# Hybrid encoder trunk: queries and keys stacked in DRAM and fetched by one ScalarE transfer per operand, and the second norm's sum moved into the second FFN pair

## The chip, the cores and the metric

The kernel runs on one core of one Trainium2 chip. The core has five engines that run side by side: TensorE (PE: matmuls; PEld: the loads of its stationary operand), VectorE (DVE), ScalarE (ACT), GpSimd (POOL) and SyncE (SP), which here only issues transfers. Transfers between DRAM and on-chip memory (SBUF) run on 16 DMA engines; SyncE, ScalarE and GpSimd can each issue them, each through a queue of its own. TensorE writes its sums to eight PSUM banks.

The metric is the device time of one execution in microseconds, the median of several runs. Lower is better.

## The reference

Two layers over a sequence of 512 positions with 1024 channels, in float32. Each layer normalises, projects, feeds three branches, merges them with gates, and ends in a gated FFN:

```python
h = rmsnorm(x, norm1_g[l])
u = h @ w_in[l]                       # q, k, v, GLU input, Fourier input
q = apply_partial_rope(rmsnorm(q, qnorm_g[l]), cos, sin)
k = apply_partial_rope(rmsnorm(k, knorm_g[l]), cos, sin)
att = diff_attention(q, k, v, lam)    # softmax of component 0 minus lam * softmax of component 1
att = rmsnorm(att, subln_g[l]) * (1.0 - lam_init)
y_a = att.reshape(b, s, WIDTH_A) @ w_proj_a[l]
...                                   # y_b: GLU, depthwise convolution, LayerNorm, swish; y_c: 2-D Fourier mixing
merged = gates[:, :, 0] * y_a + gates[:, :, 1] * y_b + gates[:, :, 2] * y_c
x = x + merged @ w_out[l]

h2 = rmsnorm(x, norm2_g[l])
f_gate, f_up = jnp.split(h2 @ w_ffn_in[l], 2, axis=-1)
x = x + (jax.nn.silu(f_gate) * f_up) @ w_ffn_out[l]
```

There are 8 heads, each with two components of 32 dimensions and 64 value dimensions. The FFN is 2816 wide.

## The kernel before

**Precision.** TensorE multiplies fast in a rounded float32 format. Each operand is therefore split into a high part and the rest (`split`, L156: a copy on ScalarE, L159, and a subtraction on VectorE, L160), and each product is three matmuls: high by high, high by low, low by high.

**Weights.** They come in chunks of 128 x 1024 (512 KB) on SyncE's queue (`chunk`, L203, tile wr), are cast to the high part on ScalarE (wh, L208), and the low part is made on VectorE (wl, L210) or, for every second chunk of the middle stages, by a cast on ScalarE (L330) and an adding transfer of GpSimd (L331). There are two buffers for the raw chunk, three for the high and four for the low part.

**Order.** The program is written as one main stream of matmuls with a running time `self.t`. Each instruction gets the due time that holds when it is written (`at`); side work such as the attention is put into a list of events with due times (`later`, `poll`) and is written between the main stream's matmuls when its time has come. A planner then puts the instructions of each engine in an order by due time and by when it holds their inputs to be ready. The order is fixed when the kernel is built; each engine runs its own in order, and the waits between engines are semaphores. Transfers belong to the order of the engine that issues them.

**Queries and keys.** `qkv` (L747) computes q, k and v with the positions on the partitions. `qk_post` (L782) normalises and rotates q and k, and `turn` (L831) transposes each group of 128 channels (two heads) and splits it into tiles at, high and low. Both parts are stored in two DRAM tensors of 128 x 512 on SyncE's queue (dqk<-at, L842). Before each head, `stack` (L850) loads for each of its two components the stacked operands: qst holds the 32 rows of the high, the low and again the high part, kst those of the high, again the high and the low part. A single matmul over 96 rows then gives the three products' sum. Each operand is three loads of 32 rows (64 KB) on SyncE's queue (L859), so there are twelve loads for each head. qst and kst have three buffers each. A load of the second component waits until the head before has finished its scores of the first component.

**Scores.** `scores` (L933) runs, for each of four query blocks, the two score matmuls into PSUM banks s (two of them), takes the maximum on VectorE (L942) and the exponential on ScalarE (L944, tile at). The attention of a layer is spread as events over the Fourier branch, the gates and the convolution branch. `drain` (L571) writes what is left of it ahead of the attention's output projection.

**Attention projection.** `gemm_two` (L237) computes the first two of eight output tiles together: the steps over the first three head pairs for both banks, then the last head pair's step for both. The banks are main, of which there are three. The other six tiles follow one by one (L580). `merge` (L680) gates each (L688) and adds it on GpSimd (L689).

**FFN.** The first FFN matrix is multiplied by a scheme of seven products instead of eight on halves of the matrices. `pair_weights` (L290) makes the seven weight operands of one of 22 pairs; `pair_gemm` (L370) runs four products, copies one bank (p15, L389 and L390) and runs the last three, on two PSUM banks that take turns: tag s for pairs 0, 3, 6 and so on, tag att for 1, 4, ..., main for 2, 5, .... So pair 3 needs the banks of pair 0. `unit` (L605) evacuates a pair: VectorE reads the banks (L608 to L614) and multiplies by rb2, the second norm's factor for each position.

**Second norm.** The square sums of x are added up on GpSimd (L416, tile acc). `inv_rms` (L419) adds them over the partitions by a matmul with ones into bank oth and computes the factor by one operation on VectorE (L426), two on ScalarE (L428, L430) and two on VectorE (L431, L432). It is written after all of pair 1 (L634), and pairs 0 and 1 are evacuated after it.

Of the kernel before, what the change touches and what calls it, by code (L numbers as in the profile page):

```python
# [9 lines left out]
F32 = mybir.dt.float32  # L10
# [6 lines left out]
P = 128  # L17
L = 2
D = 1024
T = 512  # L20
NT = T // P
KT = D // P
# [13 lines left out]
QS = ("sync",) * 4  # L36
# [21 lines left out]
LAG_N = 5000  # L58
LAG_S = 20000
LAST = (2500, 8000)  # L60
LN = (6000, 14000, 29000)
PEORD = False
CONV_LOW = -20000
# [30 lines left out]
class Hybrid:  # L94
# [139 lines left out]
        self.at(self.t)  # L234
        return ps

    def gemm_two(self, xs):  # L237
        banks = [self.bank(), self.bank()]
        n = len(xs)
        ws = [[self.wtile() for _ in xs] for _ in banks]  # L240
        for ks in (range(n - 1), (n - 1,)):
            for ps, w in zip(banks, ws):
                for k in ks:
                    wh, wl = w[k]
                    xh, xl = xs[k]
                    self.at(self.t)
                    self.mm(ps, wh, xh, k == 0, False)
                    self.mm(ps, wh, xl, False, False)
                    self.lastmm = self.mm(ps, wl, xh, False, k == n - 1)
                    self.t += 3 * PASS  # L250
                    self.poll()
        self.at(self.t)
        return banks
# [113 lines left out]
                out[n] = (hi[:, s], lo[:, s])  # L367
        return out

    def pair_gemm(self, u, w, xc, split_k=False):  # L370
        nc = self.nc
        tag = ("s", "att", "main")[u % 3]
        b1, b2 = self.bank(tag), self.bank(tag)
        h = T // 2
        n = len(xc)

        def x(name):
            return [p[name] for p in xc]

        first = (  # L380
            (b1[:, 0:h], "a11", "b11", True), (b1[:, h:T], "s1", "t1", False),
            (b2[:, h:T], "s3", "t3", True), (b2[:, 0:h], "s2", "t2", False),
        )
        steps = (list(range(n - 1)), [n - 1]) if split_k else (list(range(n)),)
        for ks in steps:
            for i, (ps, a, b, start) in enumerate(first):
                self.product(ps, w[a], x(b), ks, start and ks[0] == 0, i % 2 == 1 and ks[-1] == n - 1)
        p15 = self.slot("M")
        nc.scalar.copy(p15, b1)  # L389
        nc.vector.tensor_tensor(out=p15, in0=b2, in1=p15, op=ALU.add)  # L390
        ks = list(range(n))
        self.product(b1[:, 0:h], w["a12"], x("b21"), ks, False, False)
        self.product(b1[:, h:T], w["s4"], x("b22"), ks, False, True)
        self.product(b2[:, h:T], w["a22"], x("t4"), ks, False, True)
        return b1, b2, p15
# [153 lines left out]
    def main(self, l):  # L549
        nc = self.nc  # L550
# [15 lines left out]
        for m in range(KT):  # L566
            py = self.gemm(self.cvs)
# [6 lines left out]
        def merge_a(m, py):  # L574
            self.merge(m, ths[m], py)
            ms.append(self.split_to(merged[m], "cv" if m < 4 else "A"))

        for m, py in enumerate(self.gemm_two(self.atts)):
            merge_a(m, py)
        for m in range(2, KT):  # L580
            merge_a(m, self.gemm(self.atts))
        self.by_dma = False
        x2, xc, acc = [None] * KT, [], None
        g2 = self.par(l, "g2")
        h = T // 2
        for q in range(KT // 2):
            us = self.wtp.tile([P, 2, T], F32, tag="wth", name=self.nm("us"))
            ts = self.wtp.tile([P, 2, T], F32, tag="wtl", name=self.nm("ts"))
            for i, m in enumerate((q, q + KT // 2)):
# [4 lines left out]
                ps = self.gemm(ms)  # L594
# [3 lines left out]
                acc = self.sq_add(xt, acc, "M")  # L598
# [2 lines left out]
        self.xg, self.acc = [], None  # L601
        xin = []
        rb2 = None

        def unit(j, b1, b2, qw, scaled):  # L605
            z = self.slot("M")
            v = nc.vector.tensor_tensor
            v(out=z[:, 0:h], in0=b1[:, 0:h], in1=rb2[:, 0:h], op=ALU.mult)  # L608
            v(out=z[:, h:T], in0=b1[:, h:T], in1=qw[:, 0:h], op=ALU.add)
            v(out=z[:, h:T], in0=z[:, h:T], in1=rb2[:, h:T], op=ALU.mult)  # L610
            nc.scalar.activation(z, z, AF.Silu)
            u = self.slot("M")
            v(out=u[:, 0:h], in0=b2[:, h:T], in1=qw[:, 0:h], op=ALU.add)
            v(out=u[:, h:T], in0=qw[:, 0:h], in1=qw[:, h:T], op=ALU.add)  # L614
            if scaled:
                v(out=u, in0=u, in1=rb2, op=ALU.mult)
            v(out=u, in0=u, in1=z, op=ALU.mult)
            if j < 4:
                t = self.wtp.tile([P, 2, T], F32R, tag="wth" if j < 2 else "wtl", name=self.nm("act"))
                return self.split(u, t[:, 0, :], t[:, 1, :])  # L620
            return self.split_to(u, "att")

        done = 0
        for rnd, nj in enumerate(ROUNDS):
            act = []
            held = []
            scaled = done + nj == NJ
            for j in range(nj):
                w = self.pair_weights(done + j)
                held.append((j, *self.pair_gemm(done + j, w, xc, done + j == 0), scaled))  # L630
                if done + j == 0:
                    continue
                if done + j == 1:
                    rb2 = self.inv_rms(acc, D, "ar", "rb", True)  # L634
                while held:
                    act.append(unit(*held.pop(0)))
            done += nj
            for m in range(KT):
                if scaled and l == L - 1 and m == KT - 1:
                    self.last_tile(m, act, x2[m])  # L640
                    continue
                y = ps = self.gemm(act)
                if not scaled:
                    y = self.slot("M")
                    nc.vector.tensor_tensor(out=y, in0=ps, in1=rb2, op=ALU.mult)  # L645
                nc.vector.tensor_tensor(out=x2[m], in0=y, in1=x2[m], op=ALU.add)
                if done < NJ:
                    continue
                if l == L - 1:
                    nc.sync.dma_start(self.out[m], x2[m])  # L650
                else:
                    sc = self.dram.tile([P, T], F32, tag=f"x{l}_{m}", name=f"x{l}_{m}")
                    getattr(nc, QS[3]).dma_start(sc, x2[m])
                    xin.append(sc)
                    self.next_x(l + 1, m, x2[m])
# [126 lines left out]
    def qk_post(self, l, which, banks):  # L782
        nc = self.nc
# [3 lines left out]
        for i in range(2):  # L787
            tab = self.small(NT * 8, f"tab{i}")
            nc.vector.tensor_tensor(
                out=tab.rearrange("p (t d) -> p t d", d=8), in0=self.rope[:, i],  # L790
# [3 lines left out]
        for tt in range(NT):  # L794
# [6 lines left out]
            f = self.small(16, f"qf{tt}", 1)  # L801
            fa = self.small(16, f"qa{tt}", 1)
            nc.vector.tensor_reduce(
                out=sums, in_=sq.rearrange("p (m d) -> p m d", d=DC), axis=AX.X, op=ALU.add
# [3 lines left out]
                out=sums, in0=sums, scalar1=1.0 / DC, scalar2=EPS, op0=ALU.mult, op1=ALU.add  # L808
# [5 lines left out]
                out=q3, in0=q3, in1=f.unsqueeze(2).to_broadcast([P, 16, DC]), op=ALU.mult  # L814
# [10 lines left out]
        gc = self.small(1, f"gc{which}")  # L825
# [3 lines left out]
        out = []  # L829

        def turn(gp):  # L831
            ps = self.bank("att")
            for tt in range(NT):
                self.pin(
                    nc.tensor.transpose(  # L835
                        ps[:, tt * P : (tt + 1) * P], qs[tt][:, gp * P : (gp + 1) * P], self.ident
                    )
                )
            pair = []
            for i, src in enumerate(self.split_to(ps, "at", scale=gc)):  # L840
                d = self.dram.tile([P, T], F32, tag=f"qk{which}{gp}{i}", name=self.nm("dqk"))
                getattr(nc, QS[1]).dma_start(d, src.bitcast(F32))  # L842
                pair.append(d)
            out.append(pair)

        for gp in range(4):
            self.later(self.t + QKT + gp * 2000, "qk", lambda gp=gp: turn(gp))
# [2 lines left out]
    def stack(self, h):  # L850
        hp, h2 = divmod(h, 2)
        out = []
        for c in range(2):
            row = []
            for which, order in ((0, (0, 1, 0)), (1, (0, 0, 1))):
                dst = self.slot("kst" if which else "qst", F32R)
                lo = h2 * 64 + c * 32
                for r, hl in enumerate(order):
                    getattr(self.nc, QS[0]).dma_start(  # L859
                        dst[r * 32 : (r + 1) * 32, :].bitcast(F32), self.scr[which][hp][hl][lo : lo + 32, :]  # L860
                    )
                row.append(dst)
            out.append(row)
        return out

    def heads(self, l, t0, span):
# [45 lines left out]
        def norm(hp):  # L912
            fs[hp] = self.head_cols(atts[hp], zs.pop(hp))
            self.t += 860
# [5 lines left out]
        for u in range(NH * NT):  # L920
# [7 lines left out]
            if u % 8 == 7:  # L928
                dn, ds = (LAG_N, LAG_S) if u < NH * NT - 1 else LAST
                self.later(t + LAG_T + LAG_V + dn, "att", lambda hp=u // 8: norm(hp))  # L930
# [166 lines left out]
    def conv(self, l, t0, span):  # L1097
# [82 lines left out]
        def up(fn):  # L1180
            self.at(self.tc.cur_priority - LN_UP)
            fn()

        t1 = t0 + span + PAUSE[1]
        for fn, dt in zip((ln0, ln1, ln2), LN):
            self.later(t1 + dt, "conv", lambda fn=fn: up(fn))
# [136 lines left out]
```

## Time and profile before

| | us |
|---|---|
| median of 3 runs | 1625.27 |
| lowest and highest run | 1622.42, 1626.29 |
| the profiled execution | 1623.3 |
| its span, first to last instruction | 1621.5 |
| TensorE busy | 1593.5 |
| VectorE busy | 1309.1 |
| ScalarE busy | 870.6 |
| GpSimd busy | 183.6 |

The mean granted TensorE clock of the profiled execution is 0.993 of full speed.

The profile is of one execution. A line like L126 is the line of the kernel that issued an instruction; where a helper issues it, all its uses have that line, and the tiles (out<-in) tell them apart. PE, DVE, ACT and POOL are the engines' names in it, and a q behind a name (SPq) is the queue on which that engine issues transfers. Busy matmuls overlap, so TensorE's busy time says only that work was in it.

### The profile page before, as it was taken

What the parts mean: (1) busy time and instruction counts of PE and PEld (TensorE: products, weight loads), DVE (VectorE), ACT (ScalarE), POOL (GpSimd) and SP (SyncE); (2) the same over time, 40 slices, a digit from 0 to 9 for tenths busy, and PEclk for the clock granted to TensorE, in tenths of its full rate; (3) what the DMA queues carried; (4) which work ended last, traced back from release to release, by engine and by line L of the source; (5) the groups of instructions that cost most, each with busy time, mean ns of one, the idle gap of its engine ahead of it and who ended that gap; (6) DMA issues with size and microseconds to landing.
All of it is one profiled execution on the core that took longest, in us unless ns stands there. A gap on an engine that the chain in (4) does not pass through costs nothing.

```text
span 1621.5 us, 24447 instructions
## 1 busy us (share of the span) xinstructions
PE 1593.5 (98%) x9104; PEld 1395.3 (86%) x9104; DVE 1309.1 (81%) x2388; ACT 870.6 (54%) x1419; POOL 183.6 (11%) x162
## 2 busy tenths in 40 slices
PE   9999999999998999999999999999999899999999
PEld 7888888787888898999888888887878898989998
DVE  6999999775887786858779999996758878878684
ACT  6546556873565463535444565577635644546351
POOL 1000010113230000000100000020232300000000
PEclk9999999999999999999999999999999999999999
DMA  6556366455463554647432664554445535546361
GB/s 220 169 165 197 83 163 150 112 127 124 150 168 79 156 131 124 150 111 186 127 117 80 196 180 118 137 147 111 119 116 162 144 92 151 136 130 157 87 161 65
DMA packets 80471, 222.85 MB, mean 137 GB/s; under 512 B 11216, under 2 KB 12368, under 8 KB 80352
## 3 DMA queue, kind: packets, MB, share of 16 engines
q1 hardware_dynamic: 67392, 175.59, 34.5%
q0 software_dynamic: 12528, 45.17, 16.2%
q8 instruction: 72, 1.18, 0.3%
q10 hardware_dynamic: 432, 0.53, 0.1%
q14 instruction: 47, 0.39, 0.1%
HBM read 207.35 MB, written 13.89 MB: 136 GB/s over the span
## 4 chain that ended last, share of the span: by engine, by line
PE 92%; DVE 3%; DMA 2%; ACT 1%; issue 1%; SPq 0%; DVEq 0%; ACTq 0%
PE main L126 54%; PE s L342 10%; PE att L342 8%; PE main L342 8%; PE s L126 4%; PE att L126 3%; PE oth L126 3%; PE att L136 2%; DMA cv<-in_w 1%; DMA wr<-in_w 0%; PE att L835 0%; DVE wl L210 0%; DVE A L160 0%; DMA V<-in_xT 0%; DMA kst<-dqk 0%
## 5 line engine op out<-in xcount | busy, mean ns | idle before, releaser
L208 ACT CAST wh<-wr 128x1024 fp32r<-128x1024 f32 x178 | 186.2, 1050 | 244.2 <-PE main L126 130.5
L126 PE MATMUL main<-X,wh 128*128 128x512 f32 x864 | 278.6, 395 | 0.0
L210 DVE TENSOR_TENSOR wl<-wr,wh 128x1024 fp32r<-128x1024 f32 x138 | 176.6, 1280 | 37.6 <-ACT wh L208 37.0
L126 PEld LDWEIGHTS main<-X,wh 128*128 128x128 f32 x864 | 161.0, 189 | 32.5 <-issue 0.3
L1120 DVE SCALAR_TENSOR_TENSOR cv<-cv,hcw,cv 128x497 f32<-128x497 f32 (+14 forms) x240 | 180.4, 752 | 0.9
L126 PE MATMUL main<-X,wl 128*128 128x512 f32 x432 | 169.9, 393 | 0.0
L126 PE MATMUL main<-act,wh 128*128 128x512 f32 (+1 forms) x520 | 161.9, 391 | 0.0
L944 ACT ACTIVATE at<-s,mx 128x512 f32<-128x512 f32 x128 | 87.9, 688 | 59.0 <-DVE mx L942 50.2
L126 PEld LDWEIGHTS main<-act,wh 128*128 128x128 f32 x520 | 96.3, 188 | 21.7 <-DVE M L645 0.6
L126 PE MATMUL main<-A,wh 128*128 128x512 f32 x320 | 107.7, 393 | 0.0
L309 POOL DMA_DIRECT2D wlo<-in_w x44 | 37.8, 859 | 577.7 <-ACT wlo L308 172.9
L126 PE MATMUL main<-att,wh 128*128 128x512 f32 x320 | 100.0, 393 | 3.0 <-ACT att L159 3.0
L942 DVE TENSOR_REDUCE mx<-s 128x1 f32<-128x512 f32 x128 | 86.6, 683 | 19.3 <-PE s L126 18.7
L126 PE MATMUL main<-act,wl 128*128 128x512 f32 (+1 forms) x260 | 101.4, 391 | 0.0
L126 PE MATMUL main<-wh,X 128*128 128x512 f32 x288 | 96.7, 392 | 0.0
L126 PEld LDWEIGHTS main<-X,wl 128*128 128x128 f32 x432 | 81.5, 189 | 16.5
L331 POOL DMA_DIRECT2D wl<-in_w x40 | 34.5, 864 | 518.9 <-ACT wl L330 357.2
L126 PE MATMUL main<-cv,wh 128*128 128x512 f32 x240 | 76.8, 392 | 0.0
L126 PEld LDWEIGHTS main<-att,wh 128*128 128x128 f32 x320 | 59.7, 188 | 17.4 <-ACT att L159 3.5
L126 PE MATMUL main<-A,wl 128*128 128x512 f32 x192 | 74.4, 390 | 0.0
L126 PEld LDWEIGHTS main<-A,wh 128*128 128x128 f32 x320 | 59.7, 188 | 11.9
L126 PEld LDWEIGHTS main<-wh,X 128*128 128x128 f32 x288 | 53.8, 188 | 11.1
(371 smaller groups left out, 4206.7 us busy)
## 6 DMA issues: line engine op xcount, KB each, us to landing
wr<-in_w SPq DMA_DIRECT2D x222, 512.0 KB, 3.8
wlo<-in_w POOLq DMA_DIRECT2D x44, 512.0 KB, 5.6
wl<-in_w POOLq DMA_DIRECT2D x40, 512.0 KB, 7.6
cv<-in_w SPq DMA_DIRECT2D x80, 256.0 KB, 4.7
dqk<-at SPq DMA_DIRECT2D x32, 256.0 KB, 4.6
qst<-dqk SPq DMA_DIRECT2D x96, 64.0 KB, 2.2
kst<-dqk SPq DMA_DIRECT2D x96, 64.0 KB, 2.0
V<-in_xT SPq DMA_DIRECT2D x8, 256.0 KB, 7.1
```

Source lines behind the costliest of these rows:

```text
L126: return self.pin(self.nc.tensor.matmul(out, lhsT=lhsT, rhs=rhs, start=start, stop=stop))
L136: self.pin(self.nc.tensor.transpose(ps[:, s], src[:, s], self.ident))
L208: nc.scalar.copy(hi, raw)
L210: nc.vector.tensor_tensor(out=lo, in0=raw, in1=hi.bitcast(F32), op=ALU.subtract)
L309: nc.gpsimd.dma_start(l2, src2, accum_op=ALU.add)
L331: self.nc.gpsimd.dma_start(lo, src, accum_op=ALU.add)
L342: self.nc.tensor.matmul(ps, lhsT=a[:, s], rhs=b, start=start and k == ks[0] and i == 0, stop=last and i == 2, skip_group_check=True,)
L942: nc.vector.tensor_reduce(out=mx, in_=ps, axis=AX.X, op=ALU.max, negate=True)
L944: nc.scalar.activation(e, ps, AF.Exp, bias=mx, accum_out=z1 if c else z0)
L1120: ins = nc.vector.scalar_tensor_tensor(out=acc[:, a:b], in0=g[:, a + d : b + d], scalar=w[:, t : t + 1], in1=acc[:, a:b], op0=ALU.mult, op ...
```

## The change

Four edits.

- `gemm_two` becomes `gemm_few` with a number of banks, and is called with three: the first three output tiles of the attention projection share the steps over the first three head pairs, and the loop over the others begins at the fourth.
- `pair_gemm` takes a function `mid` that it calls after its first four products. For pair 1 this is `norm`, which writes the second norm's sum and factor with a due time 15000 before the running one (EARLY, in the same unit as `self.t`, in which a full matmul counts 216). The evacuations of pairs 0 and 1 stay where they were.
- `turn` stores one DRAM tensor of 3 x 128 x 512 for each group of 128 channels: three stores of 256 KB on SyncE's queue, of high, low, high for the queries and high, high, low for the keys.
- `stack` loads each operand by one transfer of 3 x 32 rows (192 KB) into the 96 partitions, issued by ScalarE.

```diff
+EARLY = 15000
...
-    def gemm_two(self, xs):
-        banks = [self.bank(), self.bank()]
+    def gemm_few(self, xs, few):
+        banks = [self.bank() for _ in range(few)]
...
-    def pair_gemm(self, u, w, xc, split_k=False):
+    def pair_gemm(self, u, w, xc, split_k=False, mid=None):
...
+        if mid is not None:
+            mid()
         p15 = self.slot("M")
...
-        for m, py in enumerate(self.gemm_two(self.atts)):
+        for m, py in enumerate(self.gemm_few(self.atts, 3)):
             merge_a(m, py)
-        for m in range(2, KT):
+        for m in range(3, KT):
             merge_a(m, self.gemm(self.atts))
...
+        def norm():
+            nonlocal rb2
+            self.at(self.t - EARLY)
+            rb2 = self.inv_rms(acc, D, "ar", "rb", True)
+            self.at(self.t)
...
-                held.append((j, *self.pair_gemm(done + j, w, xc, done + j == 0), scaled))
+                held.append((j, *self.pair_gemm(done + j, w, xc, done + j == 0, norm if done + j == 1 else None), scaled))
                 if done + j == 0:
                     continue
-                if done + j == 1:
-                    rb2 = self.inv_rms(acc, D, "ar", "rb", True)
...
-            pair = []
-            for i, src in enumerate(self.split_to(ps, "at", scale=gc)):
-                d = self.dram.tile([P, T], F32, tag=f"qk{which}{gp}{i}", name=self.nm("dqk"))
-                getattr(nc, QS[1]).dma_start(d, src.bitcast(F32))
-                pair.append(d)
-            out.append(pair)
+            pair = self.split_to(ps, "at", scale=gc)
+            d = self.dram.tile([3, P, T], F32, tag=f"qk{which}{gp}", name=self.nm("dqk"))
+            for r, i in enumerate((0, 0, 1) if which else (0, 1, 0)):
+                getattr(nc, QS[1]).dma_start(d[r], pair[i].bitcast(F32))
+            out.append(d)
...
-            for which, order in ((0, (0, 1, 0)), (1, (0, 0, 1))):
+            for which in range(2):
                 dst = self.slot("kst" if which else "qst", F32R)
                 lo = h2 * 64 + c * 32
-                for r, hl in enumerate(order):
-                    getattr(self.nc, QS[0]).dma_start(
-                        dst[r * 32 : (r + 1) * 32, :].bitcast(F32), self.scr[which][hp][hl][lo : lo + 32, :]
-                    )
+                self.nc.scalar.dma_start(
+                    dst[0:96, :].bitcast(F32), self.scr[which][hp][:, lo : lo + 32, :]
+                )
                 row.append(dst)
```

## The prediction

> **What bounds the kernel now.** I read first the busy table and the chain that ended last, then the list of what TensorE waited for.
>
> ```profile
> span 1621.5 us, 24447 instructions
> PE 1593.5 (98%) x9104; PEld 1395.3 (86%) x9104; DVE 1309.1 (81%) x2388; ACT 870.6 (54%) x1419; POOL 183.6 (11%) x162
> ...
> PE 92%; DVE 3%; DMA 2%; ACT 1%; issue 1%; SPq 0%; DVEq 0%; ACTq 0%
> ```
>
> TensorE is the bound: 1593.5 of 1621.5 us. The change takes no matmul away, so it can only return time that TensorE stands still or runs slowly, and can only cost time by making it stand still elsewhere. The waits of TensorE (engine, line, whom it waited for: total us, times, longest):
>
> ```profile
> PE s L342 <- DVE M L609: 8.8, 2, 4.4
> PE s L126 <- DMA kst<-dqk: 3.8, 1, 3.8
> PE main L126 <- ACT att L159: 3.0, 2, 1.5
> ```
>
> These three belong to the three edits: 8.8 us in the first FFN round (4.4 us in each layer), 3.8 us once on a load of stacked keys, 1.5 us in each layer where the attention projection waits for the last head pair. Next I asked for the stretches of these waits and those right behind them (length, then busy us of PE, PEld, DVE, ACT, POOL; the last three columns are the granted clock, the DMA share and GB/s):
>
> ```profile
> 489.20:496.00 6.80, 4.46 (x21) 4.49 (x22) 5.85 (x14) 2.29 (x3) 0.86 (x1) 0.50 0.50 77
> 1298.20:1301.60 3.40, 3.35 (x16) 3.38 (x17) 3.20 (x8) 1.21 (x1) 0.00 (x0) 0.50 0.71 134
> 1124.10:1127.50 3.40, 3.40 (x16) 3.11 (x15) 1.51 (x4) 2.28 (x5) 0.00 (x0) 0.50 0.98 178
> ```
>
> Each long wait has a second price: the granted clock is 0.50 for a while. At half the clock half of the busy time is lost: 4.46/2 = 2.2 us and 3.35/2 = 1.7 us behind the FFN waits, 3.40/2 = 1.7 us behind the key load. So the FFN waits cost 8.8 + 2.2 + 1.7 = 12.7 us, the key load 3.8 + 1.7 = 5.5 us.
>
> **The second norm's sum.** The timeline of layer 0 (start, duration, engine, line, out<-in):
>
> ```profile
> 463.41 6.15 POOL L416 TENSOR_TENSOR M<-M,M 128x512 f32<-128x512 f32 x1 [5.31 <-ACT M L411]
> 470.77 0.84 PE L342 MATMUL att<-B,A 128*128 128x256 f32 x3
> 476.06 0.40 PE L342 MATMUL att<-X,whi 128*128 128x256 f32 x2
> 480.37 1.02 PE L126 MATMUL oth<-M,ones 128*128 128x512 f32 x2
> 486.86 0.28 PE L342 MATMUL main<-B,kst 128*128 128x256 f32 x1
> 491.54 0.55 PE L342 MATMUL s<-at,whi 128*128 128x256 f32 x1 [4.40 <-DVE M L609]
> ...
> 479.29 0.69 DVE L310 TENSOR_TENSOR cv<-wr,wr 128x512 f32<-128x512 f32 x1 [3.25 <-DMA wr<-in_w]
> 488.24 0.68 DVE L432 SCALAR_TENSOR_TENSOR rb<-ar,rb 128x512 f32<-128x512 f32 x1
> 490.98 0.41 DVE L609 TENSOR_TENSOR M<-s,M 128x256 f32<-128x256 f32 x1
> 491.31 0.41 DVE L613 TENSOR_TENSOR M<-s,M 128x256 f32<-128x256 f32 x1
> ```
>
> Pair 0 writes the two s banks and is done with them at 476.06; pair 3 wants them at 486.86 + 0.12 and gets them after 491.31, because pair 0's evacuation (L608 to L613) needs rb, which is finished at 488.24 + 0.68, 8.6 us after the sum's matmul at 480.37. That matmul stands behind all of pair 1. Its input is there at 463.41 + 6.15 = 469.6. In the changed code it stands behind pair 1's first four products, which end at 471.4 (the last of them start at 470.77): 9.0 us earlier, and 1.8 us behind its input, so TensorE doesn't wait for GpSimd either. Even with the same 8.6 us, rb is ready at 480.0; the two evacuation steps that free the banks took 491.31 + 0.41 - 488.92 = 2.8 us from rb, so the banks are free at 482.8, 4.2 us before pair 3 asks. The move adds no instruction; the sum's 1.02 us of TensorE are paid at another place. EARLY lets the norm's five operations (three on VectorE like the two rows of 0.68 us, two on ScalarE with a table load) go before the weights of pairs 3 and 4; these are wanted from 487 on, and VectorE had 3.25 us without work ahead of 479.29, in which its share (2.0 us) fits. What is late next is pair 1's evacuation for pair 4, which moves forward with rb. I take the whole 12.7 us; at worst the norm is still late and nothing is saved.
>
> **Three banks instead of two.** The matmuls between the last convolution product and the last head pair's transposes (group, count | busy us, mean ns):
>
> ```profile
> L126 PE MATMUL main<-att,wh 128*128 128x512 f32 x18 | 5.6, 389 | 0.0
> L126 PE MATMUL main<-att,wl 128*128 128x512 f32 x9 | 3.5, 390 | 0.0
> ```
>
> 27 matmuls are nine for each of three banks: the planner already pulled the third output's first three steps ahead of the wait. The edit writes down what the order is, and I take 0. Its bounds are the wait itself: 3.0 us saved if the transposes come earlier, 3.0 lost if they come later.
>
> **Queries and keys.** On SyncE's queue 192 loads of 64 KB (six for each head and component) go, and 16 stores of 256 KB come. SyncE is relieved by 192 x 0.42 and charged 16 x 0.37 us; its weight loads stand behind fewer others. The third store holds an at tile by one more issue, long before the exponentials need them. ScalarE gets 64 issues.
>
> ```profile
> L859 SPq DMA_DIRECT2D kst<-dqk x96: 302/420/1777, 130.4 to 1142.3; - x96
> L842 SPq DMA_DIRECT2D dqk<-at x32: 319/368/1354, 102.1 to 940.8; - x32
> L466 ACTq DMA_DIRECT2D wraw<-in_w x2: 454/456/458, 1.2 to 1.7; - x2
> ...
> 1108.62 0.50 PE L126 MATMUL s<-kst,qst 96*128 96x512 f32 x1
> 1118.64 0.39 PE L126 MATMUL main<-X,wl 128*128 128x512 f32 x1
> 1122.85 0.47 PE L126 MATMUL s<-kst,qst 96*128 96x512 f32 x1 [3.82 <-DMA kst<-dqk]
> 1103.52 9.58 SPq L203 DMA_DIRECT2D wr<-in_w  x2
> 1113.19 3.75 SPq L859 DMA_DIRECT2D qst<-dqk  x3
> 1116.98 1.42 SPq L859 DMA_DIRECT2D kst<-dqk  x3
> ```
>
> The 3.8 us come about so: the score at 1108.62 frees the slots, but the six loads stand behind a weight load until 1113.19, and another 3.75 + 1.42 = 5.2 us are spent issuing them, up to 1118.4; TensorE's last matmul before the wait starts at 1118.64. From ScalarE's queue the two loads wait for no weight load. If they are issued within 2 us of 1108.6 they land by about 1114, well before 1118.7. I take 5.5 us off.
>
> The price is ScalarE's: 64 x 0.456 = 29 us of issue, with each second-component load waiting for a slot that a score frees. Behind it stand the exponentials (L944), the weight casts (L208, L330) and the tanh; TensorE waits for the exponentials through the two s banks, for casts only after several chunks. What cover there is:
>
> ```profile
> 140.00:300.00 160.00, 159.70 (x838) 134.85 (x837) 151.14 (x297) 97.01 (x186) 16.60 (x16) 1.00 0.55 138
> 300.00:320.00 20.00, 18.77 (x95) 15.32 (x95) 14.24 (x36) 19.58 (x31) 0.86 (x1) 1.00 0.39 95
> 1104.00:1118.00 14.00, 13.96 (x66) 11.07 (x65) 10.66 (x35) 13.19 (x25) 0.87 (x1) 1.00 0.44 100
> ```
>
> Over most of the attention ScalarE is busy 97 of 160 us and hides the issues. In the convolution's norm (300 to 320 and 1104 to 1118) it is busy 19.58 of 20 and 13.19 of 14; four issues of 0.456 us fall into each: 1.8 us a layer, 3.6 us. Bounds: 0, and the full 29 us if nothing hid them.
>
> **Sum.** The profiled execution took 1623.3 us (span 1621.5 and 1.8 around it): 1623.3 - 12.7 - 5.5 + 3.6 + 0 = 1608.7. The median of the runs, 1625.27, is 2.0 above that execution, so I forecast 1610.7, say 1611: -0.9%. With 0 for ScalarE and 3.0 from the third bank it would be 1604; with small new waits of 6 us, 1617.
>
> **Rivals.** *The loads land late.* One transfer fetches three blocks of 32 rows. Nothing in the trace shows such a shape. If its three blocks are what is spread, it runs on three DMA engines and not on sixteen.
>
> ```profile
> q1 hardware_dynamic: 67392, 175.59, 34.5%
> kst<-dqk SPq DMA_DIRECT2D x96, 64.0 KB, 2.0
> ...
> 182.26 0.71 PE L126 MATMUL s<-kst,qst 96*128 96x512 f32 x2
> 198.37 0.40 PE L126 MATMUL s<-kst,qst 96*128 96x512 f32 x1
> 1139.66 0.40 PE L126 MATMUL s<-kst,qst 96*128 96x512 f32 x1
> 1148.81 0.39 PE L126 MATMUL s<-kst,qst 96*128 96x512 f32 x1
> ```
>
> Queue q1 moved 175.59 MB in 34.5% of 16 x 1621.5 us, 19.6 KB per us and engine. 192 KB (196.6 thousand bytes) on three engines are 65.5 KB each, 3.3 us; queries and keys behind each other 6.7 us. With two issues (0.9) and the 2.0 us that a small load takes to land, 9.6 us, and more beside weight loads, against about 3.5 us on sixteen. Fourteen loads are tight (second component, heads 1 to 7 of each layer): from the score that frees the slot to the first score that needs the load there were 9.2 us (the last pair of rows, the shortest) to 15.8 us (the first pair, from the second matmul of its first row, at 182.6; the longest). The fourteen times are 9.2, 9.7, 9.9, 10.0, 10.6, 10.9, 11.2, 11.2, 12.4, 12.7, 12.8, 13.7, 13.8 and 15.8. Where a load needs 11 us TensorE stands 6 us in sum, at 13 us 22 us, at 14 us 34 us, with 1.7 us of half clock for each long one. At 11 us that is 1611 + 6 + 2 = 1619. For it: the shape, and a DMA share of 0.55 in the attention. Against it: the times left are mostly longer than 9.6 us, and the planner will place the scores anew. Since 9.6 us lies on the edge of the fourteen times, I give this and the next rival more than a third together.
>
> *The same, beyond 12 us: slower.* At 12 us the waits are 13 us and the gain is spent; at 13 to 14 us, with six to eight spells of half clock (10 to 14 us), the sum is 1611 + 32 to 48 = 1643 to 1659. It needs 2.4 us or more on top of the 9.6, for instance a ScalarE that comes late to its issue and a weight load on the same three engines.
>
> The Trainium skill, DMA: Bandwidth & Descriptors, section "Why a DMA increments its semaphore by 16 and not by 1", says that a transfer runs on the largest number of engines up to 16 that divides the outermost dimension of both sides; for 3 blocks and 96 partitions that would be three, and the sum by it 1619 or more. No transfer of the profile has an outermost dimension below 16, so no run here shows it yet.
>
> *The norm stays late.* The sum moves but rb or the evacuation is queued behind weight work on VectorE and the s banks are not free in time: the 12.7 us stay, 1611 + 12.7 = 1623. Against it are the 4.2 us of slack.
>
> *ScalarE waits in order.* SyncE's loads waited for a score for 62.5 us in 16 waits:
>
> ```profile
> SPq L859 <- PE s L126: 62.5, 16, 6.7
> ```
>
> SyncE had nothing else to do. If ScalarE stood as long, and the 63 us that it is idle between 140 and 300 didn't hide it, exponentials would come late: 62.5 us is the bound, some 10 us likely then: 1621.
>
> **Chances.** The forecast 0.50 (1603 to 1617); loads somewhat late 0.17 (1615 to 1626); loads late beyond the gain 0.20 (above 1630); norm stays late 0.08 (1620 to 1625); ScalarE waits 0.05 (1615 to 1630). What a measurement tells from no change is about 0.3%, 4.9 us: faster is below 1620.4 and slower above 1630.1. From the cases: faster 0.50 + 0.11 + 0.01 + 0.02 = 0.64; slower 0.19; same 0.17. The range 1603 to 1630 leaves out most of the slower case and little else.
>
> **What would show it.** Right: the waits on L609's successor and on kst<-dqk are gone from TensorE's list, no clock of 0.50 behind pair 3 in either layer, the ones matmul starting about 9 us before pair 2, ScalarE's convolution norm longer by some 2 us, and the wait for the attention projection still 1.5 us in each layer. Wrong: kst or qst loads on ScalarE's queue with a median landing of 5 us or more, many TensorE waits on them, or a wait of ScalarE ahead of its issues followed by TensorE waiting for L944.

## The result and the profile after

| | before | after |
|---|---|---|
| median, us | 1625.15 (4 runs, 1622.42 to 1626.29) | 1647.64 (4 runs, 1643.33 to 1650.05) |
| span of the profiled execution, us | 1621.5 | 1648.3 |
| mean granted clock of TensorE | 0.993 | 0.989 |

The ratio after to before is 1.0138, with a 95% interval of 1.0113 to 1.0163: the kernel is slower by 22.5 us. It lies outside the forecast range of 1603 to 1630 and inside the rival "The same, beyond 12 us: slower" (1643 to 1659).

First the busy table of the changed kernel, the number of its transfer packets, and the chain that ended last by engine:

```profile
span 1648.3 us, 24264 instructions
PE 1598.2 (97%) x9104; PEld 1394.5 (85%) x9104; DVE 1310.5 (80%) x2388; ACT 869.8 (53%) x1419; POOL 182.9 (11%) x162
...
DMA packets 79894, 227.02 MB, mean 138 GB/s; under 512 B 8592, under 2 KB 9744, under 8 KB 79776
...
q10 hardware_dynamic: 6768, 13.11, 2.3%
...
PE 75%; DVE 10%; DMA 9%; ACT 3%; issue 2%; ACTq 0%; POOL 0%; SPq 0%; DVEq 0%; POOLq 0%
```

The engines carry out as many instructions as before (9104, 2388, 1419 and 162); ScalarE's 64 issues are not counted as busy. What has grown are the shares of DMA and VectorE in the chain, from 2% to 9% and from 3% to 10%. (q10 is the queue on which the new loads run: it moved 0.53 MB before.) The list of TensorE's waits (engine, line, whom it waited for: total us, times, longest) says where:

```profile
PE s L127 <- DMA kst<-dqk: 25.6, 7, 7.6
PE s L127 <- issue: 7.3, 2, 3.7
PE s L127 <- ACT at L949: 3.2, 1, 3.2
PE main L127 <- ACT att L160: 3.1, 2, 1.6
```

The 8.8 us behind the FFN's evacuation are gone. One wait of 3.8 us on the stacked keys has become seven, and the two lines below it belong to such scores too. The timeline of TensorE shows them (start, duration, and in brackets the idle time and what the profile puts it down to); by the landing times in the trace, each of the ten scores starts within 0.15 us of the landing of its load of keys:

```profile
141.46 0.51 PE L127 MATMUL s<-kst,qst 96*128 96x512 f32 x1 [3.05 <-DMA kst<-dqk]
145.54 0.77 PE L127 MATMUL s<-kst,qst 96*128 96x512 f32 x1 [3.58 <-issue]
268.64 0.47 PE L127 MATMUL s<-kst,qst 96*128 96x512 f32 x1 [3.57 <-DMA kst<-dqk]
301.23 0.47 PE L127 MATMUL s<-kst,qst 96*128 96x512 f32 x1 [1.40 <-DMA kst<-dqk]
361.27 0.47 PE L127 MATMUL s<-kst,qst 96*128 96x512 f32 x1 [1.27 <-DMA kst<-dqk]
957.52 0.79 PE L127 MATMUL s<-kst,qst 96*128 96x512 f32 x1 [7.60 <-DMA kst<-dqk]
961.50 0.77 PE L127 MATMUL s<-kst,qst 96*128 96x512 f32 x1 [3.19 <-ACT at L949]
1084.52 0.47 PE L127 MATMUL s<-kst,qst 96*128 96x512 f32 x1 [3.68 <-issue]
1152.49 0.79 PE L127 MATMUL s<-kst,qst 96*128 96x512 f32 x1 [5.00 <-DMA kst<-dqk]
1183.65 0.47 PE L127 MATMUL s<-kst,qst 96*128 96x512 f32 x1 [3.72 <-DMA kst<-dqk]
```

TensorE stands 36.1 us ahead of these ten scores: 17.4 us at the first head of the two layers (the rows at 141, 145, 957 and 961) and 18.6 us at six loads of a second component. The stretches of half clock that follow (length, busy us of the five engines, then clock, DMA share and GB/s):

```profile
142.90:149.80 6.90, 4.26 (x10) 3.46 (x11) 5.38 (x12) 2.46 (x7) 0.00 (x0) 0.51 0.76 191
269.20:272.70 3.50, 3.50 (x14) 3.11 (x13) 0.64 (x1) 2.14 (x3) 0.87 (x1) 0.51 0.41 116
951.90:965.60 13.70, 4.89 (x11) 3.55 (x12) 9.99 (x20) 7.83 (x14) 0.85 (x1) 0.50 0.77 246
1085.00:1088.50 3.50, 3.50 (x12) 2.77 (x12) 3.38 (x6) 1.04 (x1) 0.00 (x0) 0.51 0.19 72
1149.90:1156.70 6.80, 4.21 (x12) 3.45 (x13) 3.16 (x6) 2.84 (x7) 0.86 (x1) 0.50 0.77 192
1184.00:1187.50 3.50, 3.50 (x10) 2.76 (x9) 2.55 (x11) 0.78 (x2) 0.00 (x0) 0.51 0.00 0
sum 37.90, PE 23.87 PEld 19.10 DVE 25.09 ACT 17.09 POOL 2.59; mean PE 3.98 PEld 3.18 DVE 4.18 ACT 2.85 POOL 0.43
```

Half of the 23.87 us that TensorE was busy in them is lost: an estimate of 11.9 us. So the stacked loads cost 36.1 + 11.9 = 48 us, where they cost 5.5 before: 42.5 us more. The FFN gave back 15.3 us (measured alone below). The balance, +27.2 us, is close to the difference of the two spans, 26.8 us. No half clock is left around pair 3 of the FFN: all six stretches lie in the attention.

When does such a load land? The page gives no landing time for the new loads. The trace has it in the counts of their completion semaphores: the 64 loads landed 5.6 to 21.3 us after their issue began, half of them after more than 10.5 us. The last pair can be followed in the timeline: its two transfers are issued at the times below, and the score that waits for them is the last row above, at 1183.65, 14.2 us after the first and 13.5 us after the second issue began.

```profile
1169.43 0.69 ACTq L864 DMA_DIRECT2D qst<-dqk  x1
1170.16 0.69 ACTq L864 DMA_DIRECT2D kst<-dqk  x1
```

The quickest of the pairs that a score waited for was issued from 351.83 on and awaited until 361.27, 9.4 us.

### The profile page after: what moved, and what is told of

It reads as the page before. It is cut to its first block, busy times and chain, and to the rows that moved or that the text cites. A ratio compares the mean times of both kernels' runs of the same rounds, so it can differ in the third digit from the quotient of the medians.

```text
span 1648.3 us, 24264 instructions
## 1 busy us (share of the span) xinstructions
PE 1598.2 (97%) x9104; PEld 1394.5 (85%) x9104; DVE 1310.5 (80%) x2388; ACT 869.8 (53%) x1419; POOL 182.9 (11%) x162
## 2 busy tenths in 40 slices
DMA packets 79894, 227.02 MB, mean 138 GB/s; under 512 B 8592, under 2 KB 9744, under 8 KB 79776
## 3 DMA queue, kind: packets, MB, share of 16 engines
q0 software_dynamic: 12528, 45.17, 15.7%
q10 hardware_dynamic: 6768, 13.11, 2.3%
## 4 chain that ended last, share of the span: by engine, by line
PE 75%; DVE 10%; DMA 9%; ACT 3%; issue 2%; ACTq 0%; POOL 0%; SPq 0%; DVEq 0%; POOLq 0%
PE main L127 41%; PE s L343 9%; PE main L343 9%; PE att L343 8%; DMA kst<-dqk 4%; PE att L127 3%; PE s L127 3%; PE oth L127 2%; DMA dqk<-at 2%; DVE cv L1125 1%; PE att L137 1%; DVE wl L211 1%; DMA wr<-in_w 1%; ACT wh L209 1%; DMA V<-in_xT 1%
## 5 line engine op out<-in xcount | busy, mean ns | idle before, releaser
L127 PE MATMUL main<-X,wh 128*128 128x512 f32 x864 | 283.9, 402 | 0.1
L127 PEld LDWEIGHTS main<-X,wh 128*128 128x128 f32 x864 | 165.1, 193 | 34.1 <-DVE M L1076 0.4
L127 PE MATMUL main<-X,wl 128*128 128x512 f32 x432 | 173.4, 401 | 0.0
L127 PE MATMUL s<-kst,qst 96*128 96x512 f32 x128 | 55.3, 435 | 36.2 <-DMA kst<-dqk 25.6
L127 PEld LDWEIGHTS main<-att,wh 128*128 128x128 f32 x320 | 59.6, 188 | 17.4 <-ACT att L160 3.5
```

Source lines behind the costliest of these rows:

```text
L127: return self.pin(self.nc.tensor.matmul(out, lhsT=lhsT, rhs=rhs, start=start, stop=stop))
```

## The experiments

The theory after this profile was that the loads are slow because of their **shape**. Their outermost dimension is the three blocks, so three DMA engines carry each. Rivals: the **order on ScalarE's queue** (loads come late because ScalarE does), and the **third store** (more bytes and more issues on SyncE ahead of the loads).

The packet count of the page speaks for the first at once. A row of 512 float32 is one packet; the short packets, under 512 B, are the ends that each engine writes when its part is done. On q10 there are 6768 - 432 = 6336 packets more than before, which is 64 loads x 99: 96 rows and three ends. The times of these packets in the trace agree: for more than half of the time that any is under way there are three at once, and there are never more than six (packets of one engine can overlap, so these counts are not exact).

**e1: the second norm alone.** The kernel before with only this:

```diff
-    def pair_gemm(self, u, w, xc, split_k=False):
+    def pair_gemm(self, u, w, xc, split_k=False, mid=None):
...
+        if mid is not None:
+            mid()
...
-                if done + j == 1:
-                    rb2 = self.inv_rms(acc, D, "ar", "rb", True)
```

> The kernel before with the move of the second norm's sum alone. If the move is worth what the changed kernel's profile says (TensorE no longer waits for pair 0's banks and the clock stays at 1.00 behind it), the time falls by 11 to 15 us, to about 1610 to 1614 us, and the 3.8 us wait on a load of kst stays. Rival: the wait was only absent in the changed kernel because everything around it was later; then the wait on the evacuation of pair 0 is still there and the time is within 5 us of before.

Measured: 1607.62 us against 1622.96 of the kernel before on the same chip, ratio 0.9895 [0.9875, 0.9914]: 15.3 us saved between the medians (the interval is 14.0 to 20.3 us), a little more than the 11 to 15 expected. A wait of 3.6 us on a load of kst stays. In its timeline the sum stands in the middle of pair 1, and pair 3 follows pair 2 without a gap:

```profile
471.27 0.62 PE L343 MATMUL att<-B,A 128*128 128x256 f32 x3
471.73 1.02 PE L127 MATMUL oth<-M,ones 128*128 128x512 f32 x2
...
477.67 0.69 DVE L435 SCALAR_TENSOR_TENSOR rb<-ar,rb 128x512 f32<-128x512 f32 x1
...
486.86 0.28 PE L343 MATMUL main<-B,kst 128*128 128x256 f32 x1
486.98 0.40 PE L343 MATMUL s<-at,whi 128*128 128x256 f32 x2
```

The factor rb is there at 478.4, 6.6 us after the sum's first matmul; pair 3 starts its first product 0.12 us after pair 2's last. This edit does what the prediction said.

**e2: the rows outermost.** The changed kernel, the same loads, the same bytes, the same queue; only the order of the source's dimensions differs, so that the 32 rows come first and the three blocks second:

```diff
-                    dst[0:96, :].bitcast(F32), self.scr[which][hp][:, lo : lo + 32, :]
+                    dst[0:96, :].bitcast(F32),
+                    self.scr[which][hp][:, lo : lo + 32, :].rearrange("r p t -> p r t"),
```

> The changed kernel with one difference: the loads name the 32 rows as the outer dimension and the three parts as the inner one, so that the 96 partitions hold the same rows in another order (the same for queries and keys). Theory one, three DMA engines: the load can be spread over sixteen engines, ScalarE's queue gets 64 x 112 packets in place of 64 x 99, the waits on second-component loads (some 26 us with their half clock) go, and the time is 1608 to 1618 us. Theory two, ScalarE's order: the waits come from transfers and exponentials queued in order on ScalarE, which this leaves as it is; the time stays above 1640 us. In between (1620 to 1640), both have a part, the second mainly at the first head of each layer.

Measured: 1603.94 us, ratio 0.9877 [0.9860, 0.9894]. Against the changed kernel that is 43.7 us between the medians (42 by the two ratios), for a rearranged pattern, and faster than the 1608 to 1618 expected. From its page: the packets, the queue of the loads, and their issues with the time to landing (KB, us):

```profile
DMA packets 80726, 227.02 MB, mean 142 GB/s; under 512 B 9424, under 2 KB 10576, under 8 KB 80608
...
q10 hardware_dynamic: 7600, 13.12, 2.7%
...
qst<-dqk ACTq DMA_DIRECT2D x32, 192.0 KB, 4.5
kst<-dqk ACTq DMA_DIRECT2D x32, 192.0 KB, 4.6
```

Now q10 has 7600 - 432 = 7168 = 64 x 112 packets more than before: 96 rows and sixteen ends. The short packets say the same, 9424 - 8592 = 832 = 64 x 13. In the trace up to 22 of q10's packets are now under way at once. The number of engines went from 3 to 16, the median landing of a load from 10.5 to 4.5 us, and the list of TensorE's waits has no line with kst left:

```profile
PE main L127 <- ACT att L160: 3.1, 2, 1.6
PE s L127 <- ACT whi L160: 1.7, 2, 0.9
...
PE s L127 <- ACT A L163: 1.4, 1, 1.4
```

**e3: the slow shape on SyncE's queue.** The changed kernel with the three blocks still outermost:

```diff
-                self.nc.scalar.dma_start(
+                self.nc.sync.dma_start(
```

> The changed kernel with the stacked loads issued by SyncE in place of ScalarE; their shape (three blocks outermost) stays. Theory one, three DMA engines: TensorE still waits on loads of kst for about as long, 1635 to 1655 us. Theory two, ScalarE's order: the waits go with the queue, 1608 to 1620 us.

Measured: 1655.62 us, 1.0194 [1.0168, 1.0219]. TensorE's list:

```profile
PE s L127 <- DMA kst<-dqk: 25.7, 9, 6.8
PE s L127 <- issue: 4.2, 1, 4.2
```

The waits on the load are as long on SyncE's queue, 25.7 us against 25.6. ScalarE's order as the cause falls, though the time lies 0.6 us above the range expected by theory one.

**e4: queries and keys alone.** The kernel before with the two parts of `turn` and `stack` and nothing else of the change.

```diff
+            d = self.dram.tile([3, P, T], F32, tag=f"qk{which}{gp}", name=self.nm("dqk"))
...
+                self.nc.scalar.dma_start(
+                    dst[0:96, :].bitcast(F32), self.scr[which][hp][:, lo : lo + 32, :]
+                )
```

> The kernel before with the edit of queries and keys alone. Both theories: it is slower than before by the attention's loss alone, 38 to 44 us, about 1663 to 1669 us; the wait for pair 0's banks (8.8 us) is there as before. If instead the edits help or hurt each other, the sum of this difference and that of the norm alone differs from the changed kernel's +22.5 us by more than 6 us.

Measured: 1662.42 us, 1.0235 [1.0194, 1.0277], 39.5 us more than the 1622.96 of the kernel before. With e1 that adds up: 39.5 - 15.3 = 24.2 us, and the whole change measured 22.5. That is additive within the noise of e4, whose two runs are 9.4 us apart. One expectation failed: the wait for pair 0's banks is 12.4 us in e4's list and not 8.8.

**e5: three loads on ScalarE.** The changed kernel with each operand in three loads of 32 rows, all 192 on ScalarE's queue, from the stacked store:

```diff
+                for r in range(3):
+                    self.nc.scalar.dma_start(
+                        dst[r * 32 : (r + 1) * 32, :].bitcast(F32), self.scr[which][hp][r, lo : lo + 32, :]
+                    )
```

> The changed kernel with each stacked load cut into three loads of 32 rows, still issued by ScalarE: 192 issues in place of 64, each over sixteen engines. Theory one, three DMA engines: the waits on kst go although ScalarE has three times the issues, 1603 to 1618 us; the excess over the rows-outer kernel is the price of 128 more issues of about 0.45 us on ScalarE (58 us of queue, nearly all hidden). Theory two, ScalarE's order: more issues on ScalarE make it worse than the changed kernel, above 1650 us.

Measured: 1608.65 us, 0.9907 [0.9887, 0.9927]. Its loads and their landing:

```profile
q10 hardware_dynamic: 9648, 13.12, 2.8%
...
qst<-dqk ACTq DMA_DIRECT2D x96, 64.0 KB, 2.8
kst<-dqk ACTq DMA_DIRECT2D x96, 64.0 KB, 2.9
```

9648 - 432 = 9216 = 192 x 48 packets: 32 rows and sixteen ends. The third store and ScalarE's queue are both still there, with three times the issues, and the kernel is fast: neither of them can be the cause of the 43 us. Three times the issues cost about 5 us: 4.6 us against e8 (below), which ran on the same chip with one issue for each operand. The size is loose, since e5 has two runs.

**e6: three banks alone.** The kernel before with `gemm_few` and three banks.

```diff
-        for m, py in enumerate(self.gemm_two(self.atts)):
+        for m, py in enumerate(self.gemm_few(self.atts, 3)):
```

> The kernel before with three banks in the attention projection alone. By the prediction, no change: the planner had the third output's first nine matmuls ahead of the wait already; the wait for the last head pair stays 3.0 us in two, the time is within 0.3% of before. Rival: the order written out saves the wait, 3 us less, with the wait gone from TensorE's list.

Measured: 1623.04 us over ten runs, 0.9998 [0.9988, 1.0008]. The wait ahead of the last head pair is what it was, but the first line of the list, the wait for pair 0's banks, has grown from 8.8 to 12.0 us although the FFN is that of the kernel before:

```profile
PE s L342 <- DVE M L609: 12.0, 2, 7.3
...
PE main L126 <- ACT att L159: 3.0, 2, 1.5
```

**e7: the good shape on SyncE's queue.** e2 with `sync` for `scalar`.

> The rows-outer kernel with its loads issued by SyncE in place of ScalarE. This asks what the queue is worth once a load runs on sixteen engines. If the 3.8 us wait of the kernel before came from loads standing behind weight loads on SyncE's queue, it is back in some form and the time is 3 to 8 us above the rows-outer kernel, 1607 to 1612 us. If the wait came from the six issues in a row alone, two issues are quick on any queue and the time equals that of the rows-outer kernel, 1602 to 1606 us.

Measured: 1608.24 us, 0.9903 [0.9888, 0.9919]. A wait on the keys comes back, and SyncE stands behind the scores (from the lists of TensorE's and of SyncE's waits). The timeline of SyncE shows the loads behind three weight loads; the score of the wait starts at 1116.10:

```profile
PE s L127 <- DMA kst<-dqk: 2.5, 1, 2.5
...
SPq L864 <- PE s L127: 71.6, 17, 6.8
...
1085.66 22.03 SPq L204 DMA_DIRECT2D wr<-in_w  x3
...
1108.38 0.59 SPq L864 DMA_DIRECT2D kst<-dqk  x1
```

Against e8 (below), which ran on the same chip with ScalarE's queue and whose other edit changed neither the wait nor the time, e7 is 4.2 us slower and no run of the one lies among those of the other. The interval overlaps that of e2, from another chip. So the queue is worth something like 4 us, of which the trace accounts for 2.5.

**e8: the last head pair earlier.** e2 with the last of the attention's events due sooner, meant to shorten the wait for the attention projection.

```diff
-LAST = (2500, 8000)
+LAST = (2500, 6000)
```

> The rows-outer kernel with the last head pair's transposes due 2000 earlier (LAST (2500, 6000) in place of (2500, 8000)). If the wait for the attention projection comes from the transposes standing behind the 27 matmuls, it shrinks from 3.1 us to below 1 us in two, 2 to 3 us less. If the planner holds the transposes' input to be late, the order and the wait stay as they are.

Measured: 1604.01 us, 0.9878 [0.9861, 0.9894]; e2 had 0.9877. TensorE's wait is the same 3.1 us in both lists (two times, at most 1.6 us).

In both kernels the transposes themselves wait for ScalarE (0.25 us in e2 at 393.83, 0.27 us in e8 at 391.22), so not the due time but the end of the attention's chain, which hands them their input, sets this wait. No gain.

The best version measured is e2: the change with its loads' rows outermost. It is 1.2% faster than the kernel before.

## Why the prediction was wrong

**The second norm's sum: right, a little small.** -12.7 us were forecast and -15.3 measured (e1). The sum's matmul moved as said, rb followed in 6.6 us rather than 8.6, and the banks were free in time. The forecast took the wait from one execution, where it was 8.8 us. In e6, which has the same FFN, it was 12.0 us, so the 2.6 us are less than the difference of this wait between these two executions.

**Three banks: right.** 0 forecast; e6 is 0.9998 with 0.1% on either side, 1.6 us.

**ScalarE's issues: probably too dear.** +3.6 us were charged for issues in the convolution's norm. e2 carries the 64 issues and is 3.7 us faster than e1, which has 192 loads on SyncE. Since e1 still has the key load's wait, put at 5.5 us with its half clock, up to some 2 us may be ScalarE's, less than the runs can tell (1602.93 to 1606.09 against 1605.90 to 1608.85). One reason is that an operation can run beside an issue, as the changed kernel's timeline of ScalarE has it:

```profile
1168.54 1.05 ACT L331 ACTIVATE wl<-wr 128x1024 fp32r<-128x1024 f32 x1
1169.43 0.69 ACTq L864 DMA_DIRECT2D qst<-dqk  x1
1169.62 0.69 ACT L949 ACTIVATE at<-s,mx 128x512 f32<-128x512 f32 x1
```

The exponential begins at 1169.62, in the middle of the issue, 0.03 us after the cast ended. It is not always so: of the 45.4 us that the 64 issues took in the changed kernel, ScalarE was busy with its own operations in 22.5 us.

**The key load: the step that failed.** The sum took 5.5 us off because two loads issued within 2 us of 1108.6 would "land by about 1114, well before 1118.7". That is the estimate for loads on sixteen engines, and this shape gets three. In the changed kernel the same two loads were issued from 1138.42 on, and the score waited for them until 1152.49: 14.1 us, and a wait of 5.0 us where 3.8 had been. Over the whole kernel the term came out at +42.5 us in place of -5.5. The prediction had this case written out as a rival and left the shape undecided ("Nothing in the trace shows such a shape"), with 0.50 for the forecast and 0.37 for the two rivals on three engines. This weighing is what was wrong.

The statement cited there, from the Trainium skill, "DMA: Bandwidth & Descriptors", section "Why a DMA increments its semaphore by 16 and not by 1", holds here: three ends for each load with the outermost dimension 3, sixteen with 32.

What was right is that the loads' place behind a weight load on SyncE's queue makes the 3.8 us. On ScalarE's queue no wait on kst is left, with one issue for each operand (e2) or three (e5); on SyncE's queue 2.5 us come back with one (e7). So it was mostly the queue, and not the number of issues.

**The load's time: right for half of the loads.** "The loads land late" added up 9.6 us for a pair: two transfers at 3.3 us, two issues and 2.0 us. The transfer itself was about right. q10 was busy 2.3% of 16 x 1648.3 us; over 64 loads that is 9.5 us of engine time each, 3.2 us on three engines (3.0 without the 0.1% that q10 had before). By the landing times in the trace, seven of the fourteen pairs of a second component landed 8.3 to 9.6 us after their first issue began and seven after 12.7 to 14.5 us. These seven met the condition that the slower rival named, 2.4 us or more on top of the 9.6. What delayed them is not shown; other traffic on the same engines is the likely part.

**The fourteen tight loads: not the whole place.** That rival's price, 1643 to 1659, took all its waits from the second components of heads 1 to 7. These gave 18.6 us of waiting and half of 3.50 + 3.50 + 4.21 + 3.50 us of half clock, 26.0 us. By itself that makes 1611 + 26 = 1637, so it is partly luck that the measured time lies in this rival's range. The other 22.0 us (17.4, and half of 4.26 + 4.89) came from the first head of each layer, which the prediction didn't look at. There all slots are empty, so the loads of three operands go out together onto the same three engines. The first three loads of keys in layer 0, with the ScalarE operation between them:

```profile
135.75 1.41 ACTq L864 DMA_DIRECT2D kst<-dqk  x2
137.26 0.69 ACT L163 ACTIVATE at<-att,gc 128x512 fp32r<-128x512 f32 x1 [8.95 <-DMA dqk<-at]
137.30 0.70 ACTq L864 DMA_DIRECT2D kst<-dqk  x1
```

They landed one after another, 5.7, 9.0 and 15.7 us after their issues; in e2 the same three took 5.5, 5.4 and 5.1 us. The scores that need the first two follow at 141.46 and 145.54. Behind such loads stores and weights are held up. These are lines of SyncE's list of waits in the changed kernel:

```profile
SPq L204 <- DMA kst<-dqk: 21.1, 4, 7.2
SPq L849 <- DMA qst<-dqk: 16.4, 4, 7.1
SPq L204 <- DMA qst<-dqk: 11.7, 2, 7.0
```

The stores of keys (L849) wait 16.4 us for loads of queries and weight loads (L204) 32.8 us for both; e2's list has no such line. The trace shows what they wait for. The transfers of SyncE and ScalarE take eight completion semaphores in turn, and in all ten of these waits SyncE's next transfer is to use the semaphore of a stacked load that has not landed yet. So a slow load of queries delays the stores of keys, these delay the loads of keys, and the first scores wait for those: from the first load of queries to the first load of keys there are 27.7 us in layer 0 and 31.9 in layer 1, in e2 23.2 and 24.2. That this chain makes the whole of the 22 us is read from the rows and was not tried by itself; that all of it goes with the shape is shown by e2.

**ScalarE waits in order: seen, and free in e2.** ScalarE does stand behind its loads: 8.95 us in layer 0 in the row above. In e2 it still stands 10.1 us in two such waits, and TensorE's list shows nothing of it.

**The norm stays late** fell with e1.

Of the signs named in advance, those of the FFN and the three banks came as "right", those of the loads as "wrong": seven waits of TensorE on kst<-dqk, and a median landing of 10.5 us where 5 us was the mark. Whether ScalarE's convolution norm became longer was not measured by itself.

What stays open: what numbers of engines between 3 and 16 would do, what the third store costs by itself (it is in all of e2, e5, e7 and e8, so it is small at most), and how much of the landing time is the other traffic on the same engines.

## What to carry to other kernels

When several transfers are merged into one, look at the outermost dimension of the new pattern before counting the issues saved: here 3 in place of 32 made a gain of 1.2% a loss of 1.4%, with the same bytes. Whether a transfer spreads could be read here from the packets of its queue (rows plus one short packet for each engine), even where the page gives no landing time. When a load may become slower, look for the place where many start at once, here the first head of a layer, before the steady state with its slots and slack.

## What the runs showed that was not expected

- An issue on ScalarE's queue took 0.69 us for 96 rows on three engines, 0.55 us on sixteen and 0.43 us for 32 rows (median of the queries' loads in the changed kernel, e2 and e5).
- A load can hold back issues on another engine's queue, of tiles that have nothing to do with it, because the two transfers share a completion semaphore: SyncE's weight loads stood 32.8 us for the stacked loads. Such waits alone need not cost much: in e5, which is fast, the weight loads stood 64.8 us for loads of kst and 26.8 us for loads of qst.
- Of the ten waits on stacked loads in the changed kernel those of 3 us and more went with half clock, with 3.5 to 4.9 us of busy time in each stretch; those of 1.27 and 1.40 us were not. The length of the wait is not all that decides: in e2 a wait of 1.57 us ends at 396.05, and the clock is 0.50 from 397.0 to 400.4.
